# Matmul with rotary embedding, one core: ten block pairs on two load paths in place of eight on one, and another order of the first loads

## The chip, the cores and the metric

The kernel runs on one core of a Trainium2 chip. The core has five engines that work side by side and wait for each other only where data or buffers make them: TensorE (PE: matmuls, and transposes as matmuls with an identity), VectorE (DVE), ScalarE (ACT), GpSimd (POOL) and SyncE (SP, which only issues transfers). Sixteen DMA engines move data between HBM and SBUF. The metric is the device time of one execution in microseconds.

## What is computed

```python
batch, seq, hidden, n_heads = (16, 512, 768, 12)      # head_dim 64
y = np.matmul(x, weight)                              # (16, 512, 768) @ (768, 768)
y = y.reshape(batch, seq, n_heads, head_dim)
y1, y2 = y[..., :32], y[..., 32:]
out1 = y1 * cos1 - y2 * sin1                          # cos, sin: (512, 64), by position
out2 = y2 * cos2 + y1 * sin2
out = np.concatenate([out1, out2], axis=-1)           # float32, (16, 512, 768)
```

`x`, the weight and the output are FP32; the kernel multiplies in FP16 and accumulates in FP32.

## The kernel before

The 8192 rows of `x` are cut into 64 tiles of 128 rows, and the tiles into 32 pairs (`n` from 0 to 31, `s` 0 or 1 in a pair). A tile has to be cast to FP16 and turned, so that `hidden` lies on the partitions, before it can be the stationary operand of a matmul. There are two ways to that.

An ordinary tile is loaded in FP32 by SP, cast by ACT into a tile `xc`, turned by six TensorE transposes into a PSUM bank `pt`, and copied back to SBUF as `xT` by ACT (the first tiles by DVE in part):

```python
def load(n, s):
    b, r = where(n, s)
    xss[n, s] = xpool.tile([P, H], FP32, tag="xs", name="xs")
    nc.sync.dma_start(out=xss[n, s], in_=x[b].rearrange("(p r) h -> r p h", r=SB)[r])

def transpose(n, s, eng):
    ...
    for t, e in CHUNKS:                                   # six chunks of 128 columns
        nc.tensor.transpose(pt[:, t, e, :], xc[:, t, e, :], ident)
    xT = tpool.tile([P, NT, 2, P], FP16, tag="xT", name="xT")
    copy(eng, xT, pt)
```

A tile of a "block pair" does without TensorE. GpSimd issues its load as four quarters that cast to FP16 on the way; each quarter puts a quarter of the columns on 32 partitions, so that what is left is to turn blocks of 32x32, which one DVE instruction does:

```python
BLOCKS = range(8, NP, 3)              # 8, 11, ... 29: eight pairs

def load_blocks(n, quarters):
    ...
    src = x[b : b + 2].rearrange("b (j a r) (q k) -> r q a (b j) k", r=SB, a=R, q=NQ)
    dst = xhs[n].rearrange("p s (j k) -> p (s j) k", j=NQ)
    for q in quarters:
        nc.gpsimd.dma_start(out=dst[ts(q, R)], in_=src[r, q])

def transpose_blocks(n, s):
    xT = tpool.tile([P, NT, P, 2], FP16, tag="xT", name="xT")
    nc.vector.transpose(out=xT.bitcast(FP32)..., in_=x16.pop((n, s)).bitcast(FP32)...)
```

A tile's product takes 12 matmuls (six chunks of `hidden`, each with 768 output columns cut at a PSUM bank's edge); a pair fills three of the six PSUM banks of `psy`. DVE multiplies each bank by cosine and sine at once into `tq` (`rope`, three instructions for a pair), GpSimd adds the two halves crosswise into `ov` (`add`, one for a pair, smaller ones at the end), and ACT or SP issues the store.

The loop over the pairs, which issues loads five to eight pairs ahead, casts two to three tiles and turns one to two tiles ahead of the matmuls:

```python
for n in range(2, NP):
    load_pair(n + AHEAD - 2)                              # AHEAD = 7
    for m, quarters in ((n + AHEAD_B, (0, 2)), (n + AHEAD_B - 1, (1, 3))):   # AHEAD_B = 8
        if m > BLOCKS[0]:
            load_blocks(m, quarters)
    for s in (0, 1):
        i = 2 * n + s
        ...
            for c in CHUNKS:
                mm(n, s, *c)
        upto("turn", i + 3 if i > 6 else 0)               # DVE or TensorE turns tile i + 2
        upto("cast", i + 5 if i > 6 else 0)               # ACT casts tile i + 4
        if n < NP - ALONE:                                # ALONE = 4: the last four pairs
            for b in ((0,), (1, 2))[s]:                   # are finished in smaller steps
                rope_bank(n, b)
            continue
        ...
```

The last four pairs are finished half a tile at a time, each half with its own `rope` and `add`; the very last half goes through DVE alone (`rope_last`).

Before the loop stands a start in which the first four tiles and the six weight chunks arrive one after the other. `warm` and `idle` are matmuls on zeros that keep TensorE busy while it waits:

```python
load_pair(0)
for k, c in enumerate(CHUNKS):
    load_w(*c)
    if k < 2:
        load(1, k)
...
warm(9)
cast(0, 0, nc.vector)
cast(0, 1, nc.scalar)
transpose(0, 0, nc.vector)
warm(2)
transpose(0, 1, nc.scalar)
warm(WARM - 11)                                           # WARM = 17
cast_w(*CHUNKS[0])
mm(0, 0, *CHUNKS[0])
mm(0, 1, *CHUNKS[0])
cast(1, 0, nc.vector)
idle(3)
transpose(1, 0, nc.scalar)
cast_w(*CHUNKS[1])
...
idle(2)
transpose(1, 1, nc.scalar)
for k, c in enumerate(CHUNKS[2:]):
    cast_w(*c)
    mm(0, 0, *c)
    mm(0, 1, *c)
    if k == 0:
        mm(1, 0, *c)
    elif k < 3:
        mm(1, 1, *CHUNKS[k - 1])
```

Of the kernel before, what the change touches and what calls it, by code (L numbers as in the profile page):

```python
# [10 lines left out]
FP32 = mybir.dt.float32  # L11
# [6 lines left out]
def kernel(  # L18
# [9 lines left out]
    nc = tc.nc  # L28
    P = nc.NUM_PARTITIONS

    B, S, H = x.shape
# [3 lines left out]
    R = 32  # L35
    NQ = P // R
    NT = H // (2 * P)
    HH = H // 2
    SB = S // P
    NP = B * SB // 2  # L40
    CHUNKS = [(t, e) for t in range(NT) for e in range(2)]
    AHEAD = 7
    AHEAD_B = 8
    ALONE = 4
    BLOCKS = range(8, NP, 3)

# [9 lines left out]
    cold = konst.tile([P, 512], FP16)  # L56
    sin_sb = konst.tile([P, SB, D], FP32)
    csn = konst.tile([P, 2, SB, D], FP32)
    w_raw = konst.tile([P, NT, 2, H], FP32)
    w_sb = konst.tile([P, NT, 2, H], FP16)  # L60

    xpool = ctx.enter_context(tc.tile_pool(name="xpool", bufs=10))
    bpool = ctx.enter_context(tc.tile_pool(name="bpool", bufs=5))
    cpool = ctx.enter_context(tc.tile_pool(name="cpool", bufs=6))
    tpool = ctx.enter_context(tc.tile_pool(name="tpool", bufs=8))
    rpool = ctx.enter_context(tc.tile_pool(name="rpool", bufs=3))
# [4 lines left out]
    xss, xhs, x16, xTT, psys, tqs, ovs = {}, {}, {}, {}, {}, {}, {}  # L71

    def copy(eng, o, i_):
        if eng is nc.scalar:
# [7 lines left out]
        nc.sync.dma_start(  # L82
            out=xss[n, s], in_=x[b].rearrange("(p r) h -> r p h", r=SB)[r]
        )

    def load_pair(n):
        for s in (0, 1):
            if n < NP and n not in BLOCKS:
                load(n, s)

    def load_blocks(n, quarters):
        if n not in BLOCKS:
            return
        b, r = where(n, 0)
# [3 lines left out]
        src = x[b : b + 2].rearrange("b (j a r) (q k) -> r q a (b j) k", r=SB, a=R, q=NQ)  # L101
        dst = xhs[n].rearrange("p s (j k) -> p (s j) k", j=NQ)
        for q in quarters:
            nc.gpsimd.dma_start(out=dst[ts(q, R)], in_=src[r, q])  # L104

    wv = weight.rearrange("(p t e) n -> t e p n", t=NT, e=2)

    def load_w(t, e, c0=0, c1=H):
        nc.sync.dma_start(out=w_raw[:, t, e, c0:c1], in_=wv[t, e, :, c0:c1])

    def cast_w(t, e, c0=0, c1=H):
        nc.vector.tensor_copy(out=w_sb[:, t, e, c0:c1], in_=w_raw[:, t, e, c0:c1])  # L112

    def cast(n, s, eng):
        xc = cpool.tile([P, H], FP16, tag="xc", name="xc")
        x16[n, s] = xc
        src = xss.pop((n, s))
        src = src.rearrange("p (m t e) -> p t m e", t=NT, e=2)
        copy(eng, xc.rearrange("p (t m e) -> p t m e", t=NT, e=2), src)

    def transpose(n, s, eng):
        xc = x16.pop((n, s)).rearrange("p (t m e) -> p t e m", t=NT, e=2)
        bank = pt_pool.tile([P, 8, P], FP16, tag="pt", name="pt")
        pt = bank[:, 0 : 2 * NT].rearrange("p (t e) m -> p t e m", e=2)
        for t, e in CHUNKS:
# [3 lines that stand above are left out]
        xTT[n, s] = xT  # L129

    def transpose_blocks(n, s):
        xT = tpool.tile([P, NT, P, 2], FP16, tag="xT", name="xT")
        nc.vector.transpose(  # L133
            out=xT.bitcast(FP32).rearrange("p t (j a) o -> p t j (a o)", j=NQ),
            in_=x16.pop((n, s)).bitcast(FP32).rearrange(
                "p (j a t) -> p t j a", j=NQ, t=NT
            ),
        )
        xTT[n, s] = xT.rearrange("p t m e -> p t e m")

# [15 lines left out]
    def mm(n, s, t, e, c0=0, c1=H):  # L156
        for k, (ps, lo, hi) in enumerate(psum(n, s)):
            a, z = max(c0, lo), min(c1, hi)
            if a >= z:
                continue  # L160
            nc.tensor.matmul(  # L161
                ps[:, a - lo : z - lo],
                xTT[n, s][:, t, e, :],
                w_sb[:, t, e, a:z],
                start=((t, e) == CHUNKS[0] and n > 1),
                stop=((t, e) == CHUNKS[-1] and (n > 1 or s >= k)),
            )
# [78 lines left out]

    def idle(k):
        for _ in range(k):
            nc.tensor.matmul(psys[1][2], cold[:, 0:P], cold, start=False, stop=False)  # L249

    ctx.enter_context(tc.manual_schedule())

    nc.vector.memset(cold, 0.0)  # L253
# [7 lines left out]
        pattern=[[-1, P]],  # L261
        channel_multiplier=1,
    )

    load_pair(0)
    for k, c in enumerate(CHUNKS):
        load_w(*c)
        if k < 2:
            load(1, k)
    nc.sync.dma_start(out=csn[:, 0], in_=cos.rearrange("(p r) d -> p r d", r=SB))  # L270
    nc.sync.dma_start(out=sin_sb, in_=sin.rearrange("(p r) d -> p r d", r=SB))
    for n in range(2, AHEAD):
# [5 lines left out]
    def upto(what, k):  # L278
        while done[what] < min(k, 2 * NP):
            n, s = divmod(done[what], 2)  # L280
            done[what] += 1
            if what == "cast":
                if n not in BLOCKS:
                    cast(n, s, nc.scalar)
            elif n in BLOCKS:
# [11 lines left out]
    cast_w(*CHUNKS[0])  # L297
    mm(0, 0, *CHUNKS[0])
    mm(0, 1, *CHUNKS[0])
    cast(1, 0, nc.vector)  # L300
    idle(3)
    transpose(1, 0, nc.scalar)
    cast_w(*CHUNKS[1])
    mm(0, 0, *CHUNKS[1])
    mm(0, 1, *CHUNKS[1])
    cast(1, 1, nc.vector)
    for c in CHUNKS[:2]:
        mm(1, 0, *c)
    idle(2)
    transpose(1, 1, nc.scalar)  # L310
    for k, c in enumerate(CHUNKS[2:]):
        cast_w(*c)
        mm(0, 0, *c)
        mm(0, 1, *c)
        if k == 0:
            mm(1, 0, *c)
# [100 lines left out]
```

## Time and profile before

| | |
|---|---|
| time, median of three (lowest to highest) | 157.2 us (157.1 to 157.7) |
| span of the profiled execution, first to last instruction | 155.4 us |
| granted TensorE clock, mean | 0.989 |
| busy: PE, DVE, POOL, ACT | 148.3, 129.6, 130.2, 75.1 us |
| moved by DMA | 49.99 MB |
| share of 16 DMA engines: SP queue, ACT queue, GpSimd queue | 46.5%, 34.3%, 16.9% |

An engine's busy time is the time in which one of its instructions was running. A chain of work is the profile's answer to what ended last: it goes back from the last instruction, at each step to what released it. A line such as L161 is a line of the kernel: L161 the matmuls, L126 the transposes on TensorE, L133 the block transposes on DVE, L175 the multiplications of `rope`, L186 the additions, L104 the loads of the block pairs, L112 the casts of the weight, L241 and L249 the matmuls on zeros.

### The profile page before, as it was taken

What the parts mean: (1) busy time and instruction counts of PE and PEld (TensorE: products, weight loads), DVE (VectorE), ACT (ScalarE), POOL (GpSimd) and SP (SyncE); (2) the same over time, 40 slices, a digit from 0 to 9 for tenths busy, and PEclk for the clock granted to TensorE, in tenths of its full rate; (3) what the DMA queues carried; (4) which work ended last, traced back from release to release, by engine and by line L of the source; (5) the groups of instructions that cost most, each with busy time, mean ns of one, the idle gap of its engine ahead of it and who ended that gap; (6) DMA issues with size and microseconds to landing.
All of it is one profiled execution on the core that took longest, in us unless ns stands there. A gap on an engine that the chain in (4) does not pass through costs nothing.

```text
span 155.4 us, 2832 instructions
## 1 busy us (share of the span) xinstructions
PE 148.3 (95%) x1090; PEld 94.5 (61%) x1090; DVE 129.6 (83%) x131; ACT 75.1 (48%) x93; POOL 130.2 (84%) x84
## 2 busy tenths in 40 slices
PE   6999999999999999999999999999999999999950
PEld 2346678666656666666666666666666666666620
DVE  0575999777798799879879879987987988999890
ACT  3422696867434563660744456266174546655200
POOL 1000599999999999899989989989998779999990
PEclk9999999999999999999999999999999999999995
DMA  5999999999999999999999999999997817896555
GB/s 145 338 416 393 398 375 342 340 398 360 363 361 377 316 397 367 312 397 336 313 355 391 280 310 412 270 309 392 338 292 239 342 63 280 324 360 257 202 202 202
DMA packets 25693, 49.99 MB, mean 322 GB/s; under 512 B 10192, under 2 KB 10704, under 8 KB 25680
## 3 DMA queue, kind: packets, MB, share of 16 engines
q1 hardware_dynamic: 10032, 26.81, 46.5%
q10 hardware_dynamic: 6944, 19.86, 34.3%
q0 software_dynamic: 8704, 3.15, 16.9%
q8 instruction: 8, 0.13, 0.3%
q14 instruction: 5, 0.04, 0.1%
HBM read 27.79 MB, written 25.17 MB: 341 GB/s over the span
## 4 chain that ended last, share of the span: by engine, by line
PE 81%; POOL 9%; DMA 2%; issue 2%; DVE 1%; POOLq 1%; ACT 1%
PE psy L161 70%; PE pt L126 9%; POOL ov L186 9%; DMA xs<-in_x_dram 2%; PE psy L241 1%; DVE tq L175 1%; PE psy L249 1%; DVE xc L77 1%; POOLq L412 1%; ACT xT L75 1%
## 5 line engine op out<-in xcount | busy, mean ns | idle before, releaser
L161 PE MATMUL psy<-w_sb,xT 128*128 128x256 f16 (+2 forms) x780 | 132.8, 323 | 0.2 <-ACT xT L75 0.2
L175 DVE TENSOR_TENSOR tq<-psy,csn 128x1024 f32<-128x1024 f32 (+1 forms) x99 | 112.0, 1174 | 14.4 <-PE psy L161 13.4
L186 POOL TENSOR_TENSOR ov<-tq 128x1536 f32<-128x1536 f32 (+2 forms) x45 | 111.5, 2504 | 4.8 <-DVE tq L175 2.7
L161 PEld LDWEIGHTS <-xT 128*128 128x128 f16 x780 | 74.2, 98 | 43.7 <-ACT xT L75 0.9
L75 ACT COPY xT<-pt 128x768 f16<-128x768 f16 x47 | 37.6, 799 | 63.2 <-PE pt L126 63.2
L75 ACT CAST xc<-xs 128x768 f16<-128x768 f32 x45 | 39.8, 906 | 5.8 <-DMA xs<-in_x_dram 5.8
L126 PEld LDWEIGHTS <-xc 128*128 128x128 f16 x288 | 20.0, 98 | 7.3 <-DVE xc L77 1.1
L126 PE MATMUL pt<-ident,xc 128*128 128x128 f16 x288 | 23.9, 219 | 0.2 <-DVE xc L77 0.2
L104 POOL DMA_DIRECT2D xh<-in_x_dram x32 | 18.8, 591 | 0.0
L325 POOL COPY mark<-xs 128x1 f32<-128x1 f32 x1 | 0.2, 185 | 16.2 <-DMA xs<-in_x_dram 16.2
L133 DVE STREAM_TRANSPOSE xT<-xh 128x384 f32<-128x384 f32 x16 | 11.3, 707 | 0.0
L241 PE MATMUL psy<-cold 128*128 128x512 f16 x17 | 6.1, 513 | 1.2 <-DVE cold L253 1.2
L77 DVE CAST xc<-xs 128x768 f16<-128x768 f32 x3 | 2.9, 953 | 4.2 <-DMA xs<-in_x_dram 4.2
L112 DVE CAST w_sb<-w_raw 128x768 f16<-128x768 f32 x6 | 3.4, 560 | 1.6 <-DMA w_raw<-in_weight_dram 1.6
L241 PEld LDWEIGHTS <-cold 128*128 128x128 f16 x17 | 1.9, 122 | 3.6 <-issue 1.9
L75 ACT ACT_TABLE_LOAD x1 | 1.3, 1283 | 0.7 <-PEq L398 0.7
L249 PE MATMUL psy<-cold 128*128 128x512 f16 x5 | 1.4, 379 | 0.0
L77 DVE COPY xT<-pt 128x768 f16<-128x768 f16 x1 | 0.6, 558 | 0.6 <-PE pt L126 0.6
L253 DVE MEMSET cold<- 128x256 uint32 x1 | 0.3, 272 | 0.9 <-PEq L398 0.9
L249 PEld LDWEIGHTS <-cold 128*128 128x128 f16 x5 | 0.5, 98 | 0.4
L216 DVE TENSOR_TENSOR ov<-psy,tq 128x384 f32<-128x384 f32 x1 | 0.6, 557 | 0.0
L212 DVE TENSOR_TENSOR tq<-psy,csn 128x384 f32<-128x384 f32 x1 | 0.6, 558 | 0.0
(9 smaller groups left out, 1.9 us busy)
## 6 DMA issues: line engine op xcount, KB each, us to landing
out_dram<-ov ACTq DMA_DIRECT2D x25, 768.0 KB, 7.5
xs<-in_x_dram SPq DMA_DIRECT2D x48, 384.0 KB, 8.2
xh<-in_x_dram POOLq DMA_DIRECT2D x32, 96.0 KB, 9.3
out_dram<-ov SPq DMA_DIRECT2D x7, 384.0 KB, 2.3
w_raw<-in_weight_dram SPq DMA_DIRECT2D x6, 384.0 KB, 7.2
out_dram<-ov SPq DMA_DIRECT2D x3, 768.0 KB, 4.9
out_dram<-ov SPq DMA_DIRECT2D x1, 192.0 KB, 2.2
out_dram<-ov ACTq DMA_DIRECT2D x1, 192.0 KB, 2.4
```

Of the source, the lines that this page charges most:

```text
L75: eng.copy(out=o, in_=i_)
L77: eng.tensor_copy(out=o, in_=i_)
L104: nc.gpsimd.dma_start(out=dst[ts(q, R)], in_=src[r, q])
L112: nc.vector.tensor_copy(out=w_sb[:, t, e, c0:c1], in_=w_raw[:, t, e, c0:c1])
L126: nc.tensor.transpose(pt[:, t, e, :], xc[:, t, e, :], ident)
L133: nc.vector.transpose(out=xT.bitcast(FP32).rearrange("p t (j a) o -> p t j (a o)", j=NQ), in_=x16.pop((n, s)).bitcast(FP32).rearrange("p ( ...
L161: nc.tensor.matmul(ps[:, a - lo : z - lo], xTT[n, s][:, t, e, :], w_sb[:, t, e, a:z], start=((t, e) == CHUNKS[0] and n > 1), stop=((t, e) ...
L175: nc.vector.tensor_tensor(out=tqs[n][:, :, c0:c1].rearrange("p j (h d) -> p j h d", d=D), in0=ps.rearrange("p (h d) -> p h d", d=D) .unsqu ...
L186: eng.tensor_tensor(out=ovs[n][:, ds(c0, w)].rearrange("p (h t d) -> p h t d", t=2, d=HD), in0=tq[:, 0].rearrange("p (h t d) -> p h t d", ...
L241: nc.tensor.matmul(psys[n][b], cold[:, 0:P], cold, start=True, stop=opened[0] < WARM - 6)
L249: nc.tensor.matmul(psys[1][2], cold[:, 0:P], cold, start=False, stop=False)
L412: with _tile.TileContext(nc) as tc:
```

## The change

Ten pairs take the way through DVE's block transpose in place of eight, and every second pair from 8 to 26 is one. Five of them (8, 12, ... 24) are loaded by GpSimd with cast as before. The other five (10, 14, ... 26) are loaded by SP, in FP32, since SP's transfers do not cast; their four quarters are issued in four successive iterations, into buffers of their own (`hpool`, two pairs), and ACT casts the tiles, into an order of columns in which DVE's transpose reads without stride. The last four pairs hold no block pair any more (before, pair 29 was one).

The weight's raw chunks move from a tensor of their own into the six buffers that the GpSimd loads use later, which makes room for `hpool`.

In the start, all four tiles of pairs 0 and 1 are loaded ahead of the weight, the first weight chunk comes in two parts (256 and 512 columns), the tiles are turned while the weight arrives, and the matmuls of pair 1 fill the steps between the chunks. The five `idle` matmuls are gone; the 17 `warm` ones stay, placed otherwise.

The purpose is to take transposes off TensorE without more work for GpSimd, and to use TensorE for products earlier.

```diff
-    BLOCKS = range(8, NP, 3)
+    BLOCKS = range(8, 25, 4)
+    BLOCKS_SP = range(10, 27, 4)
...
-    w_raw = konst.tile([P, NT, 2, H], FP32)
-    bpool = ctx.enter_context(tc.tile_pool(name="bpool", bufs=5))
+    bpool = ctx.enter_context(tc.tile_pool(name="bpool", bufs=6))
+    hpool = ctx.enter_context(tc.tile_pool(name="hpool", bufs=2))
...
-            if n < NP and n not in BLOCKS:
+            if n < NP and n not in BLOCKS and n not in BLOCKS_SP:
                 load(n, s)
...
+    def load_blocks_sp(n, q):
+        if n not in BLOCKS_SP:
+            return
+        if q == 0:
+            xhs[n] = hpool.tile([P, 2, H], FP32, tag="xf", name="xf")
+            xss[n, 0], xss[n, 1] = xhs[n][:, 0], xhs[n][:, 1]
+        load_quarter(n, q, nc.sync, xhs[n])
...
     def load_w(t, e, c0=0, c1=H):
+        if c0 == 0:
+            w_raw[t, e] = bpool.tile([P, H], FP32, tag="xh", name="w_raw")
...
     def transpose_blocks(n, s):
+        order = "p (j a t) -> p t j a" if n in BLOCKS else "p (t j a) -> p t j a"
...
-    load_pair(0)
-    for k, c in enumerate(CHUNKS):
-        load_w(*c)
-        if k < 2:
-            load(1, k)
+    for n in (0, 1):
+        load_pair(n)
+    load_w(0, 0, 0, 256)
+    load_w(0, 0, 256, H)
+    for t, e in CHUNKS[1:]:
+        load_w(t, e)
...
-    warm(9)
+    warm(10)
     cast(0, 0, nc.vector)
     cast(0, 1, nc.scalar)
     transpose(0, 0, nc.vector)
     warm(2)
     transpose(0, 1, nc.scalar)
-    warm(WARM - 11)
-    ...                                  # chunks 0 and 1, tiles of pair 1, idle(3), idle(2)
+    cast(1, 0, nc.vector)
+    cast(1, 1, nc.scalar)
+    warm(2)
+    transpose(1, 0, nc.vector)
+    warm(3)
+    for c0, c1 in ((0, 256), (256, H)):
+        cast_w(0, 0, c0, c1)
+        mm(0, 0, 0, 0, c0, c1)
+        mm(0, 1, 0, 0, c0, c1)
+        if c0 == 0:
+            transpose(1, 1, nc.scalar)
+    for k, c in enumerate(CHUNKS[1:]):
         cast_w(*c)
+        if k < 2:
+            mm(1, 0, *CHUNKS[k])
         mm(0, 0, *c)
         mm(0, 1, *c)
-        if k == 0:
-            mm(1, 0, *c)
-        elif k < 3:
-            mm(1, 1, *CHUNKS[k - 1])
+        if 1 < k < 4:
+            mm(1, 0, *CHUNKS[k])
...
-    mm(1, 1, *CHUNKS[2])
-    for c in CHUNKS[3:]:
+    for c in CHUNKS[4:]:
         mm(1, 0, *c)
+    for c in CHUNKS[:3]:
+        mm(1, 1, *c)
     upto("turn", 5)
     for c in CHUNKS[3:]:
         mm(1, 1, *c)
...
     for n in range(2, NP):
         load_pair(n + AHEAD - 2)
+        for q, ahead in ((0, 8), (2, 7), (1, 6), (3, 5)):
+            load_blocks_sp(n + ahead, q)
```

More of the change, by code (lines that the diff above doesn't have):

```diff
@@ L69 @@
     py_pool = ctx.enter_context(tc.tile_pool(name="py", bufs=6, space=bass.MemoryType.PSUM))
-    xss, xhs, x16, xTT, psys, tqs, ovs = {}, {}, {}, {}, {}, {}, {}
+    w_raw, xss, xhs, x16, xTT, psys, tqs, ovs = {}, {}, {}, {}, {}, {}, {}, {}
     def copy(eng, o, i_):
@@ L87, in load_pair, with load_quarter @@
         for s in (0, 1):
-            if n < NP and n not in BLOCKS:
+            if n < NP and n not in BLOCKS and n not in BLOCKS_SP:
                 load(n, s)
+    def load_quarter(n, q, eng, dst):
+        b, r = where(n, 0)
+        src = x[b : b + 2].rearrange("b (j a r) (q k) -> r q a (b j) k", r=SB, a=R, q=NQ)
+        dst = dst.rearrange("p s (j k) -> p (s j) k", j=NQ)
+        eng.dma_start(out=dst[ts(q, R)], in_=src[r, q])
     def load_blocks(n, quarters):
@@ L96, in load_blocks @@
             return
-        b, r = where(n, 0)
         if quarters[0] == 0:
@@ L100, in load_blocks @@
             x16[n, 0], x16[n, 1] = xhs[n][:, 0], xhs[n][:, 1]
-        src = x[b : b + 2].rearrange("b (j a r) (q k) -> r q a (b j) k", r=SB, a=R, q=NQ)
-        dst = xhs[n].rearrange("p s (j k) -> p (s j) k", j=NQ)
         for q in quarters:
-            nc.gpsimd.dma_start(out=dst[ts(q, R)], in_=src[r, q])
+            load_quarter(n, q, nc.gpsimd, xhs[n])
+    def load_blocks_sp(n, q):
[5 more added lines that the diff above has]
+        load_quarter(n, q, nc.sync, xhs[n])
     wv = weight.rearrange("(p t e) n -> t e p n", t=NT, e=2)
     def load_w(t, e, c0=0, c1=H):
-        nc.sync.dma_start(out=w_raw[:, t, e, c0:c1], in_=wv[t, e, :, c0:c1])
+        if c0 == 0:
+            w_raw[t, e] = bpool.tile([P, H], FP32, tag="xh", name="w_raw")
+        nc.sync.dma_start(out=w_raw[t, e][:, c0:c1], in_=wv[t, e, :, c0:c1])
     def cast_w(t, e, c0=0, c1=H):
-        nc.vector.tensor_copy(out=w_sb[:, t, e, c0:c1], in_=w_raw[:, t, e, c0:c1])
+        nc.vector.tensor_copy(out=w_sb[:, t, e, c0:c1], in_=w_raw[t, e][:, c0:c1])
     def cast(n, s, eng):
@@ L134, in transpose_blocks @@
             out=xT.bitcast(FP32).rearrange("p t (j a) o -> p t j (a o)", j=NQ),
-            in_=x16.pop((n, s)).bitcast(FP32).rearrange(
-                "p (j a t) -> p t j a", j=NQ, t=NT
-            ),
+            in_=x16.pop((n, s)).bitcast(FP32).rearrange(order, j=NQ, t=NT),
         )
@@ L244, in warm @@
             opened[0] += 1
-    def idle(k):
-        for _ in range(k):
-            nc.tensor.matmul(psys[1][2], cold[:, 0:P], cold, start=False, stop=False)
     ctx.enter_context(tc.manual_schedule())
@@ L284, in upto @@
                     cast(n, s, nc.scalar)
-            elif n in BLOCKS:
+            elif n in BLOCKS or n in BLOCKS_SP:
                 transpose_blocks(n, s)
@@ L295 @@
     transpose(0, 1, nc.scalar)
-    warm(WARM - 11)
-    cast_w(*CHUNKS[0])
-    mm(0, 0, *CHUNKS[0])
-    mm(0, 1, *CHUNKS[0])
     cast(1, 0, nc.vector)
[L301 to L307, printed above, removed]
-        mm(1, 0, *c)
-    idle(2)
-    transpose(1, 1, nc.scalar)
-    for k, c in enumerate(CHUNKS[2:]):
+    cast(1, 1, nc.scalar)
[9 more added lines that the diff above has]
+    for k, c in enumerate(CHUNKS[1:]):
         cast_w(*c)
+        if k < 2:
+            mm(1, 0, *CHUNKS[k])
         mm(0, 0, *c)
         mm(0, 1, *c)
-        if k == 0:
-            mm(1, 0, *c)
-        elif k < 3:
-            mm(1, 1, *CHUNKS[k - 1])
+        if 1 < k < 4:
+            mm(1, 0, *CHUNKS[k])
     nc.vector.tensor_copy(out=csn[:, 1, :, 0:HD], in_=sin_sb[:, :, HD:D])
```

## The prediction

> **What bounds the kernel now.** I read the busy shares by slice first. TensorE is at 9 in every slice but the first and the last, at full granted clock; DVE and GpSimd are lower but close, and the DMA engines are full until four fifths of the span.
>
> ```profile
> PE   6999999999999999999999999999999999999950
> DVE  0575999777798799879879879987987988999890
> POOL 1000599999999999899989989989998779999990
> DMA  5999999999999999999999999999997817896555
> ```
>
> So the second view is the waits. If another engine were the bound, TensorE would wait for it. It waits for next to nothing, and it is DVE that waits for TensorE:
>
> ```profile
> DVE tq L175 <- PE psy L161: 13.4, 20, 0.9
> ...
> PE psy L161 <- ACT xT L75: 0.2, 1, 0.2
> ```
>
> Third, the chain that ended last (start, length, what), for what TensorE's time is made of:
>
> ```profile
> 10.59 0.82 PE psy L161 x4
> 11.41 0.43 PE psy L249 x2
> 11.85 0.34 PE pt L126 x6
> 12.18 4.88 PE psy L161 x30
> 17.06 0.34 PE pt L126 x6
> ...
> 80.45 0.34 PE pt L126 x6
> 80.79 5.85 PE psy L161 x36
> ...
> 133.79 1.06 POOL ov L186
> ```
>
> From 10.59 us to the end of the products, near 149.9, TensorE is full. An ordinary tile costs it 0.34 for six transposes and 1.95 for twelve matmuls (5.85 for 36), so an ordinary pair costs 2 x 2.29 = 4.57 us and a block pair 3.90. At 133.79 the chain leaves TensorE for GpSimd: the last additions run one behind the other, some 0.8 us after what they need.
>
> Fourth, DVE's order of time around the block pair at 82.55 to 84.89, to see how much room it has. The bracket gives the idle time before a row and who ended it:
>
> ```profile
> 84.89 3.46 DVE L175 TENSOR_TENSOR tq<-psy,csn 128x1024 f32<-128x1024 f32 x3
> 88.75 3.68 DVE L175 TENSOR_TENSOR tq<-psy,csn 128x1024 f32<-128x1024 f32 x3 [0.40 <-PE psy L161]
> 93.32 2.35 DVE L175 TENSOR_TENSOR tq<-psy,csn 128x1024 f32<-128x1024 f32 x2 [0.89 <-PE psy L161]
> ```
>
> In the 13.04 us of one period of three pairs (82.55 to 95.59) it idles 0.40 + 0.89 and is busy 11.65 by the view of stretches.
>
> **What the Trainium skill says.** "TensorE: Matmul & The Clock Gate", section Back-to-back issue gap, gives N/2.4 + 2.5 ns for a warm matmul of N columns. A transposed chunk (N = 128) is then 56 ns, six are 0.335 us; a chunk's 512 and 256 columns are 0.325, a tile's 1.95. The chain agrees: 0.34 and 1.95. "DMA: Bandwidth & Descriptors", section SWDGE vs HWDGE vs iDMA, says that a cast during a transfer is only to be had from GpSimd's queue. This agrees with the kernel: its FP16 landings are all on that queue. It is why SP's quarters must land in FP32 and cost ACT a cast. The same page, section Issuing engines are not separate DMA queues, says that all queues run on the same 16 engines and interleave. The three queue shares before (46.5, 34.3, 16.9%) do add up to one nearly full set, so moving a load to SP saves GpSimd's time, not the DMA engines'. "VectorE: DVE Perf Modes", section The three transpose paths, says that DVE turns blocks of 32x32 only; that is why these loads come in quarters. One such instruction is 707 ns here.
>
> **The change, part by part.**
>
> *Transposes.* Before, 16 tiles pass TensorE by and 48 do not (288 transposes / 6); after, 20 and 44. Four tiles less by 0.335 is 1.34 us, all on the path, since TensorE is full where they stood.
>
> *DVE in exchange.* Four more block transposes. In the sequence above, one moves the next instruction by 0.61 to 0.62 (82.55 to 83.16, 84.27 to 84.89), so two are 1.23, and one of the nine multiplications of a period is (11.65 - 1.23) / 9 = 1.158. The new period is two pairs: TensorE 4.57 + 3.90 = 8.47; DVE 6 x 1.158 + 1.23 = 8.18. It fits with 0.29 to spare, where the old period had 1.4 in 13. Also inside the period: taking the end of a pair's matmuls as zero, DVE does two multiplications (to 2.36), the first turn (2.98), one multiplication (4.1), the second turn (4.7). TensorE wants the turned tiles at 4.24 and 6.52. So there is over 1 us for either and no wait.
>
> *GpSimd.* Its issue of a quarter is 0.59:
>
> ```profile
> L104 POOL DMA_DIRECT2D xh<-in_x_dram x32 | 18.8, 591 | 0.0
> ```
>
> Twelve of 32 go: 7 us less work, off the path except at the end. For two pairs it then needs 2 x 3.43 + 2 x 0.59 = 8.04 in 8.47.
>
> *ACT.* Six more casts (54 tiles in place of 48) of 0.91 against four fewer copies of 0.80: some 2 us more on an engine that is 48% busy. Nothing.
>
> *Start.* The bound there is the arrival of the weight, one chunk per microsecond. The last chunk's cast, in DVE's order of time:
>
> ```profile
> 13.77 0.56 DVE L112 CAST w_sb<-w_raw 128x768 f16<-128x768 f32 x1 [0.45 <-DMA w_raw<-in_weight_dram]
> ```
>
> The bytes up to there are the same after, so I keep 14.33 for it. Before, TensorE is behind at that point: 18 of the 30 matmuls from 12.18 on come ahead of the last chunk's, which starts at 12.18 + 18 x 0.163 = 15.1. The two zero matmuls at 11.41 and the late tile of pair 1 (turned at 11.85) put it there. From 15.1 it has 12 matmuls (1.95), a transposed tile (0.34) and six matmuls (0.98) until pair 1 is complete: 18.4. After, each chunk's arrival releases three tile-chunks of 0.325, 0.98 per 1.0 us. So TensorE keeps pace and can begin the last chunk at 14.33. What then remains is 0.65 + 0.65 + 1.95 (pair 0's last chunk, two for the third tile, all six for the fourth) + 0.34 = 3.6: 17.9. Gain 0.45 us. The dropped `idle` matmuls (0.65 + 0.43 in the chain) are not counted again: they stood in gaps that the chunks set anyway.
>
> *End.* With pair 29 ordinary, TensorE spends 18.3 instead of 17.6 us on the last four pairs (this is in the 1.34 already). GpSimd's fifteen small additions there take 15 x 0.96 = 14.4, so it catches up and the 0.8 of lag goes. Then DVE's `rope_last` and its store end the kernel. In the trace before, that store lands at 153.7 and the last one behind GpSimd at 154.3, so about 0.5 us is gained.
>
> Sum: 1.34 + 0.45 + 0.5 = 2.3 us of 157.2, which gives 154.9.
>
> **The rivals.**
>
> *DVE becomes the bound.* For it: 8.18 of 8.47 is 97%. Against it: the durations of its instructions hardly vary through the trace, and SP's tiles are turned without stride. If it took 5% longer, a period would be 8.6 and the nine and a half periods would give back 1.2 us: 156.1.
>
> *A load comes late.* The DMA engines are full to 120 us. An FP32 quarter writes twice the bytes of a cast one, in rows of 768 bytes onto 32 partitions. If that is slow (say at half the rate of the 384 KB loads), the engines get some 8 us more work.
>
> ```profile
> xh<-in_x_dram POOLq DMA_DIRECT2D x32, 96.0 KB, 9.3
> ```
>
> That is the median to landing; the longest early ones took 17. Pair 12's last quarters would be issued near 39 us and be turned near 58. That is 19 us against 17, the thinnest margin I see. For the others: in the trace before, loads end near 119 us, 17 ahead of their use, and SP's new loads are free to run seven pairs ahead. A late pair would cost 1 to 3 us once: 156 to 158.
>
> *The start goes the other way.* The first product now waits for the fifth transfer rather than the third. If the weight lands half a microsecond later than I assume, the start's gain is gone: 155.4.
>
> *More than I count.* If the start keeps TensorE fuller and GpSimd is clear at the end, 153.8.
>
> **Range and chances.** The 1.34 is nearly certain; start and end together are 0.95, give or take 0.6; a stall of DVE or of a load takes up to 2 with a chance of perhaps one in five. So 154.9, with 153.9 to 156.4. Faster by 2% needs 154.06 or less, 0.85 more than I sum: 0.15. Slower by 2% needs a stall that repeats: 0.04.
>
> **What would show it.** TensorE's share stays full and its transposes are 264; the chain alternates 3.90 of matmuls in a row with tiles of 2.29 every two pairs; DVE's waits for TensorE fall from 13.4 us to about 4; the last cast of the weight still starts near 13.8 and pair 1 ends near 17.9; the end of the chain leaves TensorE for DVE, not GpSimd. It is wrong if TensorE's products wait for DVE or for a transfer inside the loop, if the multiplications' 1.2 us grow, or if the weight lands late.

## The result, and the profile after

The changed kernel takes 155.24 us (median of four, 155.02 to 155.44), the kernel before 157.45 beside it (157.10 to 157.81). The ratio is 0.986, with a 95% interval of 0.983 to 0.989: 2.2 us or 1.4% less. The prediction said 154.9, a gain of 2.3.

The span of the profiled execution goes from 155.4 to 153.0 us. Two moments in the traces split these 2.4: the last product ends at 149.89 before and at 148.24 after (1.65 less), and from there to the end of the span it takes 5.51 before and 4.76 after (0.75 less).

The busy shares by slice of the kernel after, to be laid beside those of before:

```profile
PE   6999999999999999999999999999999999999970
...
DVE  0656999777798998989898989989898987987991
...
POOL 1000399999997999799997999787897879899990
...
DMA  4999999999999999999999999999999937896555
```

TensorE is still at 9 in every slice but the ends, and the DMA engines are still at 9 to four fifths of the span. The shares of the three large DMA queues add up to 98.1% of 153.0 us (54.7 + 32.9 + 10.5), where they were 97.7% of 155.4.

The waits of the kernel after (who, for whom, us in total, times, longest). DVE still waits for TensorE, and TensorE's longest entry for DVE is that of two weight chunks in the start:

```profile
DVE tq L188 <- PE psy L174: 11.5, 19, 1.0
...
PE psy L174 <- DVE w_sb L126: 0.4, 2, 0.2
```

The chain that ended last (start, length, what), cut to the start, one and a half periods of the loop, and the end. Line L174 is now the matmuls, L140 the transposes on TensorE:

```profile
4.63 6.97 DMA w_raw<-in_weight_dram
...
11.63 0.57 DVE w_sb L126
...
12.24 4.45 PE psy L174 x26
16.69 0.34 PE pt L140 x6
17.02 1.77 PE psy L174 x12
...
75.24 5.85 PE psy L174 x36
81.09 0.34 PE pt L140 x6
81.42 1.95 PE psy L174 x12
83.38 0.34 PE pt L140 x6
83.71 5.85 PE psy L174 x36
...
148.75 0.57 DVE psy L225
...
149.34 0.56 DVE ov L229
```

From one row of 5.85 to the next are 8.47 us, the period of two pairs that was predicted: an ordinary pair of 4.57 and a block pair of 3.90. The end no longer goes through GpSimd. DVE's own last rows are the end, at 149.90, and GpSimd's last addition, which ended at 151.8 before, now ends at 149.5, just ahead of them.

DVE's order of time over two periods, the first with a block pair of SP's (`xc`), the second with one of GpSimd's (`xh`); the bracket is the idle time ahead of a row:

```profile
49.32 2.35 DVE L188 TENSOR_TENSOR tq<-psy,csn 128x1024 f32<-128x1024 f32 x2 [0.40 <-PE psy L174]
51.59 0.57 DVE L148 STREAM_TRANSPOSE xT<-xc 128x384 f32<-128x384 f32 x1
52.08 1.19 DVE L188 TENSOR_TENSOR tq<-psy,csn 128x1024 f32<-128x1024 f32 x1
...
57.79 2.36 DVE L188 TENSOR_TENSOR tq<-psy,csn 128x1024 f32<-128x1024 f32 x2 [0.67 <-PE psy L174]
60.06 0.70 DVE L148 STREAM_TRANSPOSE xT<-xh 128x384 f32<-128x384 f32 x1
60.69 1.18 DVE L188 TENSOR_TENSOR tq<-psy,csn 128x1024 f32<-128x1024 f32 x1
...
66.26 2.36 DVE L188 TENSOR_TENSOR tq<-psy,csn 128x1024 f32<-128x1024 f32 x2 [0.41 <-PE psy L174]
```

In each period DVE waits once for TensorE: 0.67 after SP's pair, 0.41 after GpSimd's. So it is busy 7.80 and 8.06 of 8.47. It has room, but half a microsecond of it.

What did change its kind is what holds back SP. First SP's queue before, then after:

```profile
SPq L82 <- ACT xc L75: 72.3, 31, 5.0
```

```profile
SPq L99 <- DMA xs<-in_x_dram: 17.4, 9, 4.2
SPq L83 <- DMA xs<-in_x_dram: 15.1, 13, 3.3
SPq L83 <- DMA xf<-in_x_dram: 14.5, 10, 2.4
SPq L99 <- DMA out_dram<-ov: 10.5, 5, 3.5
```

Before, SP waited for buffers: a new load was issued when ACT had cast the tile that lay in its place. After, it waits for earlier transfers to land, loads and stores alike. The transfers' records say how: those of SP and ACT together report their landings on eight semaphores in turn, and GpSimd's on eight others. In every run here a transfer is issued only when the one before it on its semaphore has landed, so that SP and ACT never have more than eight under way. In the stretch from 40 to 100 us they have 4.5 under way on average before and 7.8 after. The experiments with all pairs on SP show where that leads.

### The profile page after: what moved, and what is told of

The parts are those of the page before. It is cut to its first block, busy times and chain, and to the rows that moved or that the text cites. A ratio compares the mean times of both kernels' runs of the same rounds, so it can differ in the third digit from the quotient of the medians.

```text
span 153.0 us, 2768 instructions
## 1 busy us (share of the span) xinstructions
PE 146.4 (96%) x1062; PEld 92.8 (61%) x1062; DVE 129.9 (85%) x136; ACT 76.8 (50%) x95; POOL 123.6 (81%) x72
## 3 DMA queue, kind: packets, MB, share of 16 engines
q1 hardware_dynamic: 15040, 29.17, 54.7%
q10 hardware_dynamic: 6944, 19.86, 32.9%
q0 software_dynamic: 5440, 1.97, 10.5%
## 4 chain that ended last, share of the span: by engine, by line
PE 86%; DMA 5%; DVE 4%; SPq 2%; issue 1%; DVEq 0%
PE psy L174 77%; PE pt L140 9%; DMA w_raw<-in_weight_dram 5%; DVE tq L188 3%; SPq L123 1%; SPq L83 1%; DVE w_sb L126 0%; DVE psy L225 0%; DVE ov L229 0%; DVE tq L225 0%; DVEq L229 0%; DVEq L188 0%
## 5 line engine op out<-in xcount | busy, mean ns | idle before, releaser
L174 PE MATMUL psy<-w_sb,xT 128*128 128x256 f16 (+2 forms) x781 | 132.0, 323 | 0.4 <-DVE w_sb L126 0.4
L188 DVE TENSOR_TENSOR tq<-psy,csn 128x1024 f32<-128x1024 f32 (+1 forms) x99 | 111.9, 1169 | 12.1 <-PE psy L174 11.5
L174 PEld LDWEIGHTS <-xT 128*128 128x128 f16 x781 | 74.6, 98 | 44.9 <-ACT xc L76 0.5
L76 ACT COPY xT<-pt 128x768 f16<-128x768 f16 x42 | 33.6, 800 | 53.4 <-PE pt L140 53.4
L76 ACT CAST xc<-xs 128x768 f16<-128x768 f32 x42 | 36.8, 904 | 12.3 <-DMA xs<-in_x_dram 11.0
L140 PEld LDWEIGHTS <-xc 128*128 128x128 f16 x264 | 18.1, 98 | 6.7 <-DVE xc L78 1.5
L140 PE MATMUL pt<-ident,xc 128*128 128x128 f16 x264 | 21.8, 219 | 0.3 <-DVE xc L78 0.2
L99 POOL DMA_DIRECT2D xh<-in_x_dram x20 | 11.8, 595 | 0.5 <-issue 0.5
L76 ACT CAST xc<-xf 128x768 f16<-128x768 f32 x10 | 9.1, 906 | 0.0
L254 PE MATMUL psy<-cold 128*128 128x512 f16 x17 | 6.2, 515 | 1.2 <-DVE cold L261 1.2
L148 DVE STREAM_TRANSPOSE xT<-xh 128x384 f32<-128x384 f32 x10 | 7.0, 701 | 0.0
L148 DVE STREAM_TRANSPOSE xT<-xc 128x384 f32<-128x384 f32 x10 | 5.6, 562 | 0.0
L126 DVE CAST w_sb<-w_raw 128x768 f16<-128x768 f32 (+2 forms) x7 | 3.4, 500 | 2.2 <-DMA w_raw<-in_weight_dram 2.2
```

The lines of the kernel that those rows point to most:

```text
L76: eng.copy(out=o, in_=i_)
L99: eng.dma_start(out=dst[ts(q, R)], in_=src[r, q])
L126: nc.vector.tensor_copy(out=w_sb[:, t, e, c0:c1], in_=w_raw[t, e][:, c0:c1])
L148: nc.vector.transpose(out=xT.bitcast(FP32).rearrange("p t (j a) o -> p t j (a o)", j=NQ), in_=x16.pop((n, s)).bitcast(FP32).rearrange(orde ...
L174: nc.tensor.matmul(ps[:, a - lo : z - lo], xTT[n, s][:, t, e, :], w_sb[:, t, e, a:z], start=((t, e) == CHUNKS[0] and n > 1), stop=((t, e) ...
L188: nc.vector.tensor_tensor(out=tqs[n][:, :, c0:c1].rearrange("p j (h d) -> p j h d", d=D), in0=ps.rearrange("p (h d) -> p h d", d=D) .unsqu ...
```

## The experiments

Each kernel below was timed beside the kernel before, which took 157.3 to 157.4 us in the median, so 0.001 of a ratio is 0.16 us. Ratios leave out executions over 1.5% above the shortest of the same kernel, so where a kernel spreads widely the ratio lies below what its median gives, and the profiles of the kernels "all by GpSimd" and "all by SP, stores by GpSimd" are of such longer executions. A gap of TensorE is given as the time from one instruction's start to the next, less the usual spacing of the two (0.06 to 0.22 us); the idle time in a bracket is 0.15 to 0.2 us less.

### The terms of the sum

**The start alone.** The kernel before with the new order of the first loads, casts and matmuls; block pairs as before.

```diff
-    load_pair(0)
-    for k, c in enumerate(CHUNKS):
-        load_w(*c)
-        if k < 2:
-            load(1, k)
+    for n in (0, 1):
+        load_pair(n)
+    load_w(0, 0, 0, 256)
+    ...                    # and the casts, turns and matmuls of the new start
```

> The kernel before with the new start alone (eight block pairs on GpSimd as before). My sum gives the start 0.45 us, and the two traces show pair 1 complete at 18.0 in place of 18.4: 157.0 beside 157.4 of before. Since pair 29 is still a block pair, GpSimd's lag at the end stays. Rival: the start is worth nothing by itself, because GpSimd's additions, which begin when the first block loads are issued, set the end (chain before): 157.4.

Measured: 157.19 us in the median, ratio 0.9988 (0.9981 to 0.9995). That is 0.2 us, of the 0.4 expected. Its chain:

```profile
12.08 4.45 PE psy L161 x26
...
133.35 1.06 POOL ov L186
```

In the profiled execution, the shortest of this kernel, the last product ends 0.45 earlier than before (149.44), just what the step "Start" says. This kernel still ends through GpSimd, whose chain begins at 133.35, where it began at 133.79: 0.44 earlier as well. So in this execution the 0.45 comes through. Over the executions the gain is 0.1 to 0.3, and why it is less there isn't shown.

**The blocks alone.** The changed kernel with the old start, `idle` matmuls included.

```diff
-    for n in (0, 1):
-        load_pair(n)
-    load_w(0, 0, 0, 256)
-    ...
+    load_pair(0)
+    for k, c in enumerate(CHUNKS):
+        load_w(*c)
+        if k < 2:
+            load(1, k)
```

> The changed kernel with the start of before (five zero matmuls and the old order of loads). My sum: 1.34 us for four tiles off TensorE and 0.5 for the end, so 155.6 beside 157.4 of before. Rival: block pairs and start need each other, then this one comes to less than 1.3 us of gain.

Measured: 156.21 us in the median (155.48 to 157.18), ratio 0.9931 (0.9905 to 0.9958): 1.1 us, of the 1.8 expected. The two shortest executions (155.48 and 155.57) agree with the sum and the others don't, so something happens in some executions that isn't in the sum. In the profiled one (156.15) TensorE has a gap of 0.32 us at 107.3. ACT's order of time there:

```profile
105.84 0.38 ACTq L244 DMA_DIRECT2D out_dram<-ov  x1
106.31 1.72 ACT L76 CAST xc<-xs 128x768 f16<-128x768 f32 x2 [3.35 <-DMA xf<-in_x_dram]
```

ACT was idle 3.35 us ahead of a cast. The cast's own data had landed some 14 us before. What waited was the store in front of it (105.84), issued as soon as the quarter before it on its semaphore had landed (issued 94.18, landed 105.76). So a late quarter can hold back a store, and a store that isn't issued holds back ACT's casts and copies behind it.

The two halves add up to 1.3 us (0.2 + 1.1), the whole change gives 2.0 to 2.2. About 0.8 us belongs to neither alone; by the intervals of the ratios this is uncertain by some 0.5 us.

**The changed kernel once more**, as a base beside the next three.

```diff
 (no edit)
```

> The changed kernel unaltered, as the measure beside the others of this set. My sum: 2.3 us under before, near 155.1. If the late loads that held the ten-pairs-by-SP kernel back also touch this one now and then, its times spread by more than those of before (0.8 us) and the middle is 155.5 or more.

Measured: 155.38 us (155.13 to 155.78), ratio 0.9873 (0.9852 to 0.9894). Both measurements of it agree.

**A block pair back among the last four.** The last of SP's pairs is 30 in place of 26. The count of transposes stays.

```diff
-    BLOCKS_SP = range(10, 27, 4)
+    BLOCKS_SP = (10, 14, 18, 22, 30)
```

> The changed kernel with its last SP block pair moved from 26 to 30, into the last four. TensorE has the same work in all. My term for the end: with a block pair among the last four TensorE spends 0.67 less there, GpSimd's fifteen additions end later than DVE's last half again, 0.5 us: 155.7. Rival: the shorter end of the changed kernel has nothing to do with where the pairs lie: 155.2.

Measured: 156.10 us (155.75 to 156.21), ratio 0.9911 (0.9893 to 0.9929): 0.7 us over the changed kernel. The last product ends at 148.56 (0.32 later), and 5.4 us follow it in place of 4.76. The chain turns to GpSimd again, at 132.47. GpSimd's last additions in order of time, in the kernel before, in the changed kernel, and here:

```profile
133.79 18.00 POOL L186 TENSOR_TENSOR ov<-tq 128x768 f32<-128x768 f32 x17 [0.29 <-POOL ov L186]
...
131.47 18.00 POOL L199 TENSOR_TENSOR ov<-tq 128x768 f32<-128x768 f32 x17 [0.56 <-POOL ov L199]
...
132.47 18.01 POOL L199 TENSOR_TENSOR ov<-tq 128x768 f32<-128x768 f32 x17 [0.97 <-POOL ov L199]
```

In all three GpSimd takes 18.0 us for its last seventeen additions and never waits in between. What the place of the block pairs sets is when these 18.0 us begin, and how long TensorE takes beside them: 18.3 us for four ordinary pairs, 17.6 with a block pair among them. With four ordinary pairs DVE's last row comes behind GpSimd's (149.90 and 149.48), with a block pair it comes ahead of it (150.22 and 150.47). So the step "End" has its cause shown.

### The margins of DVE and GpSimd

**DVE with 0.8 us more in each block pair.** A zeroing of a tile that nobody reads stands ahead of the two turns.

```diff
 def transpose_blocks(n, s):
+    if s == 0:
+        nc.vector.memset(junk, 0.0)          # 128 x 768, FP32
```

> The changed kernel with 0.8 us of DVE work more (a memset of an unused tile) ahead of each block pair's turns. In the trace DVE is busy 8.07 and 7.80 us in periods of 8.47. With 0.8 more it needs 8.73 on average, 0.26 over, in nine and a half periods: 1.5 to 2.5 us longer, 156.7 to 157.7. Rival, DVE is already the bound: ten times 0.8, 163. Rival, DVE has room in plenty: 155.2.

Measured: 157.06 us, ratio 0.9984 (0.9974 to 0.9993): 1.7 us over the changed kernel, and inside what was expected. In DVE's order of time the added row takes 0.70 and moves the next one by 0.61, and the wait for TensorE is gone:

```profile
60.52 0.70 DVE L148 MEMSET junk<- 128x768 f32 x1
61.13 0.61 DVE L151 STREAM_TRANSPOSE xT<-xh 128x384 f32<-128x384 f32 x1
61.66 1.19 DVE L191 TENSOR_TENSOR tq<-psy,csn 128x1024 f32<-128x1024 f32 x1
```

DVE is now busy 8.49 of a period of 8.60. In the loop that costs little: the last product ends at 148.80, 0.56 later. The larger part comes behind it: 6.4 us instead of 4.76 to the end of the span. DVE and with it GpSimd come late to the last four pairs, the chain leaves for GpSimd at 131.02, and GpSimd's last addition ends at 150.77, 1.29 later. The last stores, now issued close together, take 3.3 us to land instead of 2.0. So DVE's room is 0.4 to 0.7 us a period, and its loss shows mostly at the end. The expected size came out, but not by the path expected, 0.26 us in each period.

**All ten pairs loaded by GpSimd.** It tells what SP's part of the loads is good for.

```diff
-    BLOCKS = range(8, 25, 4)
-    BLOCKS_SP = range(10, 27, 4)
+    BLOCKS = range(8, 27, 2)
+    BLOCKS_SP = ()
```

> The same ten block pairs, all loaded by GpSimd with cast, none by SP. TensorE has the same work. GpSimd then needs 2 x 3.43 + 4 x 0.59 = 9.2 us for two pairs against TensorE's 8.47, up to the last load near pair 19, and DVE may run only three pairs ahead of it: 159 to 163. Rival: GpSimd's issues are hidden anyway and SP's part is only bookkeeping: 155.2.

Measured: ratio 1.0158 (1.0128 to 1.0188), near 159.9 us: slower than before the change. From its waits:

```profile
DVE tq L188 <- POOL ov L199: 6.4, 13, 0.5
PEld L174 <- DVE xT L148: 6.1, 7, 0.9
```

The wait goes down the line: DVE for GpSimd's additions, TensorE for the tiles that DVE turns. TensorE waits once in each period, and from one such wait to the next it is 9.14 to 9.20 us in this trace. GpSimd's own sum is 2 additions of 3.43 and four issues of 0.595: 9.24. With ten pairs on it, GpSimd is the bound; with five it is busy 7.95 to 8.09 of 8.47 in the changed kernel.

### The loads

**All ten pairs loaded by SP.** Buffers for four pairs instead of two; the first two quarters of pair 8 are issued before the loop.

```diff
-    BLOCKS = range(8, 25, 4)
-    BLOCKS_SP = range(10, 27, 4)
-    hpool = ctx.enter_context(tc.tile_pool(name="hpool", bufs=2))
+    BLOCKS = ()
+    BLOCKS_SP = range(8, 27, 2)
+    hpool = ctx.enter_context(tc.tile_pool(name="hpool", bufs=4))
```

> The same ten block pairs, all loaded by SP in FP32 and cast by ACT, none by GpSimd (four FP32 buffers). TensorE-bound theory: no difference, 155.2 (GpSimd and DVE have a little less to do). Rival, the loads: after the change the loads already land only 6 to 12 us ahead of their cast in the loop (before: 20 us and more), SP waits for landings and ACT once stood 2.6 us behind a store; with twenty more transfers TensorE would wait for ACT, 156 to 159.

Measured: 157.72 us in the median (156.26 to 159.59), ratio 1.0016 (0.9997 to 1.0034). The rival was right: the gain is gone. TensorE has gaps of 0.52 at 103, 0.47 at 112 and 1.51 at 133. The time by which a landing precedes its cast falls from 6.8 to 0.1 us in the loop, until casts wait:

```profile
ACT xc L76 <- DMA xf<-in_x_dram: 5.1, 4, 1.9
ACT xc L76 <- DMA out_dram<-ov: 3.4, 2, 1.8
```

The first two gaps follow casts that ran 0.07 us after their quarters landed. Ahead of the third the data was there, and ACT stood behind a store (130.97) that waited for another store to land (130.89).

So neither path carries ten pairs: GpSimd has no time for them, and SP's loads come late. Five and five stays below both limits.

Why are they late? Two readings. By the first, a *number in flight* limits: SP and ACT together have at most eight transfers under way, and the quarters double the number of SP's transfers for a pair. In the trace before, the first transfers from SP's queue (issued, landed):

```
 0.74   4.33      3.06   9.80      6.73  14.10
 1.18   5.30      3.73  10.78      7.90  14.47
 1.65   6.71      4.35  11.76      8.87  15.45
 2.12   7.88      4.85  12.74
 2.59   8.85      5.63  13.75
```

The ninth (4.85) is issued only after the first has landed (4.33), the tenth (5.63) after the second (5.30), the next three 0.02 us after the third, fourth and fifth. By the second reading the *rate* of the DMA engines limits: they are full, and an FP32 quarter occupies them for longer per byte. (By the shares of SP's queue before, 46.5% of 155.4 us, after, 54.7% of 153.0, and with all pairs on SP, 67.1% of 155.5, some 1.5 to 1.7 times as long as the queue's other transfers; an estimate.) Three kernels were to tell these apart.

**All by SP, ordinary pairs in one transfer each.** From pair 7 on 768 KB instead of two of 384: fewer transfers, the same bytes. The ten buffers of a tile become five of a pair.

```diff
-        for s in (0, 1):
-            if n < NP and n not in BLOCKS and n not in BLOCKS_SP:
-                load(n, s)
+        ...                                  # one buffer for the pair; up to pair 6 as before
+            nc.sync.dma_start(
+                out=pair, in_=x[b : b + 2].rearrange("b (p r) h -> r p b h", r=SB)[r]
+            )
```

> The kernel with all ten block pairs on SP (157.7, and TensorE waited at 103, 112 and 133 us for ACT), with one change: from pair 7 on an ordinary pair is loaded by one transfer of 768 KB in place of two of 384. Bytes are the same, transfers fewer by about twenty-five. If it was the number of transfers in flight (SP and ACT waiting for a landing before they may issue the next one) that made loads late and held ACT behind its stores: 155.2 to 156. If it was the DMA engines' rate: 157.7 again.

Measured: 163.85 us in the median, ratio 1.0297 (1.0272 to 1.0321). Neither reading said so. SP waits most of all for stores:

```profile
SPq L110 <- DMA out_dram<-ov: 46.3, 14, 7.5
```

A store issued at 99.33 lands at 109.37; the quarter behind it on its semaphore is issued at 109.39 and lands at 116.25; the cast that needs it runs at 116.32, and the next store is issued behind that cast at 116.45. Loads and stores hold each other up, and TensorE has gaps of 2.4, 0.9 and 2.4 us.

**All by SP, stores by GpSimd.** The kernel with ten pairs on SP and 384 KB loads, but the loop's stores are issued from GpSimd's queue, so that they can't hold SP's loads or ACT's casts.

```diff
-    store(n - 3, nc.scalar)
+    store(n - 3, nc.gpsimd)
```

> All ten block pairs on SP, and the stores of the loop issued by GpSimd in place of ACT. Bytes and transfers are those of the kernel with all ten on SP (157.7). If loads and stores held each other up there, because SP's and ACT's transfers together may have only some eight unlanded (SP waited 20 us for stores to land, ACT's casts stood behind stores that waited for loads), this parts them: 155.0 to 155.8. If the DMA engines' rate is what makes the loads late: 157.7 again. If GpSimd's issues (25 by about 0.6 us, 7.2 + 0.6 x 2 in 8.47 us for two pairs) become the bound: over 158.

Measured: 160.64 us in the median (158.19 to 162.56), ratio 1.0107 (1.0061 to 1.0152). GpSimd isn't the bound (129 us busy of 160.8). SP no longer waits for stores, but the median from issue to landing grows from 8.7 to 11.5 us for tiles and from 9.0 to 12.1 for quarters. The loads are later than with the stores on ACT.

**Both together.**

```diff
+    (loads as in the kernel with whole pairs)
+    store(n - 3, nc.gpsimd)
```

> All ten block pairs on SP, the loop's stores on GpSimd, and an ordinary pair loaded by one transfer of 768 KB. With stores on GpSimd and 384 KB loads (160.6) SP's issues followed landings one by one: eight transfers unlanded, each 12 to 14 us on its way, is 0.6 per us where 0.71 are needed. With whole pairs five transfers per 8.47 us are needed, 0.59 per us. If the number in flight is the limit: 155.2 to 156.5, no stall of TensorE on a load. If it is the rate at which the DMA engines carry SP's bytes beside the stores: 160 again.

Measured: 159.23 us in the median, ratio 1.0083 (1.0061 to 1.0104), with gaps of TensorE of 1.14, 0.83 and 1.26 at 95, 104 and 114 us. With fewer transfers and the stores out of the way the loads should have come early if only the number counted. They didn't, which speaks for the rate; SP still waited some 40 us for landings (16.5 us in the median for a whole pair, 13.7 for a quarter).

What the DMA engines moved tells more. The view of stretches has it in its last column, in GB/s, behind the DMA engines' share (the times ahead of them are the busy times of the five engines). From 40 us on in this kernel:

```profile
40.00:60.00 20.00, 20.00 (x145) 12.69 (x143) 18.18 (x19) 11.98 (x16) 19.14 (x11) 1.00 1.06 332
60.00:80.00 20.00, 20.00 (x140) 12.58 (x139) 18.67 (x21) 11.00 (x14) 19.58 (x9) 1.00 1.05 357
80.00:100.00 20.00, 19.02 (x138) 11.91 (x137) 17.81 (x18) 10.70 (x13) 18.35 (x11) 1.00 1.05 345
```

The mean of these three stands below with that of other kernels, beside what a period of the loop asks for (an estimate: its loads and stores over its length, with all pairs on SP two pairs in and two out, 3.15 MB in 8.47 us) and the bytes under way (from the issue and the landing of every transfer):

| 40 to 100 us | asked for, GB/s | moved, GB/s | under way, MB |
|---|---|---|---|
| before | 332 | 349 | 2.9 |
| after | 348 | 351 | 3.6 |
| all by SP | 371 | 341 | 2.9 |
| all by SP, both together | 371 | 345 | 4.1 |

With all quarters on SP the loop asks for more than the engines move, so the lead of the loads is used up, and two fifths more bytes under way add 1%. So it is the rate that limits, as far as these four show it, and the changed kernel sits just below it. The limit of eight does something else: it passes a late landing on to the next transfer of its semaphore, a store too, and through a store in ACT's order to ACT's casts and copies.

### A better version

**Pairs 4 and 6 as block pairs of SP's too**, which takes four more tiles off TensorE. Their quarters are issued before the loop, in place of the ordinary loads of these pairs.

```diff
-    BLOCKS_SP = range(10, 27, 4)
+    BLOCKS_SP = (4, *range(6, 27, 4))
```

> The changed kernel with two block pairs more, 4 and 6, on SP, where DVE idles about 0.9 us per pair. TensorE-bound theory: four tiles less by 0.335, 1.34 us: 154.0. Rival, the loads: eight more quarters in a stretch in which the DMA engines are full and TensorE follows the loads by 2 to 5 us: nothing gained or worse, 155.3 to 157.

Measured: 159.0 us in the median (156.9 to 162.6), ratio 1.0023 (1.0000 to 1.0045). The waits name the loads again:

```profile
ACT xc L76 <- DMA xs<-in_x_dram: 16.3, 8, 5.0
```

Up to pair 11 many casts do follow their landings by 0.1 to 0.2 us, and TensorE loses nothing there. It has gaps of 0.87, 1.03 and 0.99 us at 92, 101 and 111 us, far from the pairs that were changed, and there the tiles' data had landed 5 to 9 us before their casts. Ahead of the first gap the copy that TensorE needs runs at 90.66, after 2.01 us in which ACT was idle. It stands behind a store (90.19), and the store waited for the load before it on its semaphore (issued 78.86, landed 90.11). The other two gaps are alike (stores at 99.70 and 109.17, landings at 99.62 and 109.10). So here it isn't a load of TensorE's own that comes late. Leads are 3 to 5 us shorter at these places than in the changed kernel; that this is what lets landings come behind the stores' turn is likely, and not shown.

**Pair 6 as a block pair of GpSimd's.**

```diff
-    BLOCKS = range(8, 25, 4)
+    BLOCKS = (6, *range(8, 25, 4))
```

> The changed kernel with an eleventh block pair, 6, loaded by GpSimd in the time in which it has no additions yet (its wait is for tile 4 and not tile 6, so its issues fall near 15.4 us). No transfer is added to SP, two of 384 KB go. TensorE loses two tiles' transposes: 0.67 us, 154.6. Rival: the loads in the first 30 us are the limit there, and cast quarters take the DMA engines longer than the tiles they replace, so TensorE waits near pair 6 or 7: 155.2 or more.

Measured: 155.25 us in the median (154.63 to 156.17), ratio 0.985 (0.980 to 0.990): not to be told from the changed kernel. Three of the six executions took 154.6 to 154.8, as the sum says, and three 155.7 to 156.2. The profiled one is of the longer ones (156.09): two transposed tiles are saved, and a gap of 1.3 us appears at 46.2, when pair 8's last quarter, issued at 20.73, has only just landed (45.31):

```profile
45.44 0.70 DVE L148 STREAM_TRANSPOSE xT<-xh 128x384 f32<-128x384 f32 x1 [2.43 <-DMA xh<-in_x_dram]
```

No version here beats the changed kernel for certain.

## Why the prediction was right, and where it wasn't

- **Transposes, 1.34: right.** 264 are left, and the chain's period is 8.47 as worked out.
- **Start, 0.45: right in its path, 0.3 to 0.45 measured.** The steps are those of the prediction. By the records of the single matmuls the products of the last three chunks begin at 12.24, 13.22 and 14.26, each 0.05 to 0.06 us behind the end of its chunk's cast:

```profile
11.63 0.56 DVE L126 CAST w_sb<-w_raw 128x768 f16<-128x768 f32 x1 [0.43 <-DMA w_raw<-in_weight_dram]
12.61 0.56 DVE L126 CAST w_sb<-w_raw 128x768 f16<-128x768 f32 x1 [0.42 <-DMA w_raw<-in_weight_dram]
13.64 0.56 DVE L126 CAST w_sb<-w_raw 128x768 f16<-128x768 f32 x1 [0.47 <-DMA w_raw<-in_weight_dram]
```

  So TensorE keeps pace and begins the last chunk at 14.26 (14.33 predicted), with hardly any time to spare: a chunk's products take 0.98 us, and the casts start 0.98 to 1.03 apart. In the chain these steps are one row from 12.24 on, because TensorE's waits of 0.01 and 0.06 us are shorter than the overlap of two matmuls in the records. Pair 1 is complete at 18.00 (17.9 predicted) and was at 18.37 before, a gain of 0.37. In the whole kernel the last product is 1.65 earlier, which leaves 0.31 beside the transposes' 1.34.
- **End, 0.5: right, though GpSimd does not catch up.** The profiles have 0.75 less behind the last product (5.51 to 4.76). Of these, 0.52 is the predicted term: before, GpSimd's last store landed at 154.26, 0.52 behind DVE's at 153.74; after, it lands ahead of DVE's (151.45 and 151.96). The rest is DVE's store, which lands a little sooner, and the last moments of the span. But GpSimd's additions still run one behind the other to 149.48, so only 0.4 us lie between its end and DVE's. The pair-at-the-end experiment brings GpSimd's lag and 0.7 us back.
- **DVE, 8.18 of 8.47: right, with 0.1 to 0.4 more room.** It is 8.06 with GpSimd's tiles and 7.80 with SP's, since their turn reads without stride (562 ns against 701). The rival "DVE becomes the bound" was nearly true: 0.7 us more of DVE's time takes most of the gain away.
- **DVE's waits "fall from 13.4 to about 4": wrong.** They are 11.5. Inside the periods they are 5.4 in ten waits, 0.40 and 0.67 in turn where 0.29 was worked out. The other 6.1 stand in ordinary pairs ahead of pair 8 and behind pair 26; the prediction left those out.
- **GpSimd, 8.04: right** (8.09 and 7.95 in two stretches of 8.47), and with ten pairs its sum of 9.24 became the period.
- **"SP's new loads are free to run seven pairs ahead": wrong, without cost here.** SP waits for landings instead. From pair 15 on the lead of a landing over its cast was 20 to 26 us before and is 9 to 16 after, up to pair 27; it doesn't shrink along the loop. ACT's order of time shows how near a stall comes all the same:

```profile
104.49 0.38 ACTq L244 DMA_DIRECT2D out_dram<-ov  x1
104.97 0.92 ACT L76 CAST xc<-xs 128x768 f16<-128x768 f32 x1 [2.62 <-DMA xs<-in_x_dram]
```

  The bracket names the cast's data, but that had landed some 15 us earlier. The store in front of it was issued at 104.49, when one of SP's quarters (issued at 92.41) had landed at 104.41. TensorE had no gap from these 2.62 us. Twice the quarters, or two early pairs more, and it has. The rival "a load comes late" is therefore near the real edge of this design, but the prediction looked for it elsewhere: GpSimd's quarters for pair 12, its "thinnest margin", landed at most 11.2 us after their issue, the last at 50.53, and were turned from 60.06 on. And a landing need not be late for its own cast to do harm: a store that waits for it is enough.
- **The sum, 2.3: 2.2 measured, but its terms aren't independent.** Start alone gives 0.2 and blocks alone 1.1. One part of the gap is seen: with the old start a quarter held up a store and TensorE lost 0.32. Why the old start should shift the transfers so was not tried, and the rest of the 0.8 stays open.
- **The spacing of matmuls: right, by a formula for another case.** The section that the prediction names, Back-to-back issue gap in "TensorE: Matmul & The Clock Gate" of the Trainium skill, gives N/2.4 + 2.5 ns for an isolated matmul, and for a stream of weight loads and matmuls about 81 ns at 128 columns and 131 at 512. In both traces here, where every matmul has its own weight load, the spacing in the stream is 56 and 216 ns. So the formula holds here, and the figures for a stream do not.

## What to carry to other kernels

A way around a full engine has a capacity of its own, and two ways used by half can both stay inside it: five pairs on GpSimd and five on SP gain 2.2 us, where ten on either lose it all. Work out the period of every engine that gets the work, and for transfers the bytes that a period asks for against what the DMA engines move, because their share is full either way; where they ask for too much, the lead from landing to first use shrinks until it is gone. When an engine waits for data that landed long ago, look at the transfer in front of it in its order of work. And look at what happens behind the last product: here a DVE without room showed it there more than in the loop.

## What the runs showed of the hardware

- DVE's turn of 128x384 (FP32 words) takes 562 ns when it reads without stride and 701 ns when it reads every third word; the next instruction is moved by 0.49 and 0.63 us.
- Under this load a transfer of 192 KB in rows of 768 bytes to 32 partitions takes no less time from issue to landing than one of twice the size to 128 partitions (median, in the changed kernel):

```profile
xs<-in_x_dram SPq DMA_DIRECT2D x44, 384.0 KB, 9.7
xf<-in_x_dram SPq DMA_DIRECT2D x20, 192.0 KB, 11.6
```

- With these quarters among the transfers the full DMA engines move 341 to 351 GB/s (means of 40 to 100 us). When the changed kernel's last quarter has landed (104.41) and tiles of 384 KB and stores are left, they move 408 to 416 in the four slices from 107 to 122 us.
- In these programs a transfer of SP or ACT waits until the one before it on its semaphore has landed: a store by ACT at 104.49 for a load of SP's landed at 104.41, and in one kernel 46.3 us of SP's waits for stores. Eight semaphores serve the two; whether the chip could have more under way was not tried. An issue that stands in ACT's order of work holds ACT's computing too, up to 3.35 us here.
